# Attention of the second sequence: three of each head's four key blocks transposed by VectorE and a trip through DRAM, in place of two

## The chip, the cores and the metric

The kernel runs on one core of one Trainium2 chip. The time is device microseconds of one execution, the median over runs. Before the change it is 2035.41 us, with three runs from 2034.75 to 2035.72 us.

A core has five engines, each with an instruction stream of its own that runs in order: TensorE (PE, with its weight loads PEld), VectorE (DVE), ScalarE (ACT), GpSimd (POOL) and SyncE (SP). They wait for one another through semaphores. DMAs are issued by an engine (here by SP and POOL) and land later.

## The reference

Two sequences of 512 tokens by 1024 channels go through one encoder layer each, with the same weights: half a step of a SwiGLU network, a token mixer, half a step of a second SwiGLU network, and a final norm. The mixer is the part that matters here:

```
proj = h @ w_in
aq, ak, av, mq, mk, mv, gate_pre, o_pre, g_att, g_mlstm = jnp.split(proj, split_at, axis=-1)
...
att = gqa_block_attention(aq, ak, av)          # 8 heads, 2 key/value heads, head size 64
mem = mlstm_bidirectional(mq, mk, mv, gate_pre, mlstm_gate_bias, o_pre, mlstm_head_norm)   # 4 heads
merged = jax.nn.sigmoid(g_att) * (att @ w_up_att) + jax.nn.sigmoid(g_mlstm) * (mem @ w_up_mlstm)
x = x + merged @ w_out
```

and in the attention, for each block of 128 queries and each head,

```
s = jnp.einsum('bqkgd,bskd->bkgqs', qi, k, preferred_element_type=jnp.float32) * scale
p = jax.nn.softmax(s, axis=-1).astype(v.dtype)
return jnp.einsum('bkgqs,bskd->bqkgd', p, v)
```

The probabilities `p` come out with the query on the partitions. The product with `v` sums over the keys, so it needs them with the key on the partitions: 512 by 512 probabilities of each head have to be transposed. This transposition is what the change touches.

## The kernel before

**Precision.** Every float32 matrix product is done as three matmuls: an operand is split into a high and a low half (`split`, L713: ACT writes the high half, L715, DVE the rest, L716), and high by high, high by low and low by high are summed in PSUM.

**Weights.** A weight unit is loaded and split once, for the first sequence, and both halves are parked in DRAM (`wpark`). The second sequence only reads them back: `load_w` issues two DMAs on SP (L293), of 512 KB each, high and low, into one of four slots `w`. With few exceptions the list of work units (`go`, `fill`) issues a unit's loads some units ahead of its matmuls.

**The mixer of the second sequence**, `mix(1, ...)`. The projections for queries and keys come first. Then the attention runs as a loop over eight heads h and four slots b. In slot b of iteration h the code does, in this order: `score(h + 1, b)`, i.e. two score matmuls for query block b of the *next* head (L1101), a maximum on DVE (L1104), the exponential on ACT (L1106), a reciprocal on DVE (L1107) and the scaling (L1109 on ACT or L1111 on DVE); some filler matmuls (`among`, L825, single matmuls of gate projections that nothing in the attention waits for); the transposition of key block b of head h; more fillers; and `values`, two matmuls (L1148) of the key block that was transposed one slot earlier, with its high half and then its low half. Eight fillers stand in every slot, 7 and 1 in slot 0, 5 and 3 in the others. After the fourth key block of a head, ACT and DVE drain the accumulator `pso` into `f` (L1162, L1163), and every second head splits it into `att`.

A key block is transposed in one of two ways:

- By PE, `turn_keys`: four 128x128 transposes (L1117) write one PSUM bank `pst`, and `parts` splits the bank into `t` tiles (L715, L716). In the first sequence all four key blocks go this way, in the second key blocks 2 and 3, whose values come first (`KBS`).
- By DVE and DRAM, only in the second sequence, key blocks 0 and 1: `turn_early` lets DVE transpose 32x32 squares (L1129, one instruction for each query block of 128 by 256 values) into the tile `box`. `send` writes `box` to DRAM (`abuf`) with four DMAs on SP (L1133) in slot 1. `fetch`, in slots 0 and 1 of the *next* iteration, reads one key block back by a DMA that POOL issues (L1138), in such an order that the whole block comes out transposed, into a tile `f`; `parts` splits that as above.

After the loop stands a tail: key blocks 0 and 1 of head 7 are fetched and multiplied. Around them the program places the value projection of the mLSTM (L804; 96 matmuls for four accumulators, three in the `mm` banks and one in the `pso` bank, evicted to `Vm` by L1009 on ACT and L866 on DVE). Then come the four heads of the mLSTM, each with the same kind of trip by DVE and DRAM: exponentials (L1306) of `box` tiles that are loaded on SP (L1071, `box<-ebuf`) and added to a table (L1074), products with the scores `qk` (L1292, L1308), transposes on DVE (L1330), eight sends on SP (L1334, `tbuf`), and later the closing matmuls (`mem_out`, L1360). Heads 0 and 1 are prepared first, then the closing matmuls of head 0 run, and so on, with work units for PE between them. `proj_w` (L839) does the attention's merge, in units of 24 or 12 matmuls that share a weight load.

**What sets the order.** Most of the attention's matmuls are pinned in the order of the code (`pin`). A scheduler of the framework places all other instructions on each engine by priorities and its own estimates of time. `t` tiles rotate through 11 buffers, `f` tiles through 4; PSUM has three `mm`, one `pso`, two `pss` and two `pst` banks.

## Time and profile before

| | us |
|---|---|
| median of three runs | 2035.41 |
| profiled execution, its own time | 2037.6 |
| span of the profiled execution | 2035.8 |
| PE busy in the span | 2020.2 |
| DVE busy | 1584.0 |
| ACT busy | 921.5 |
| POOL busy | 111.1 |

The granted clock of the profiled execution is 0.999. The span runs from the first to the last recorded instruction; 1.8 us of the execution's own time lie outside it.

How it is read: a row of the timeline begins with the start in us and the length, then the engine, the line, the operation and the tiles as output<-input with buffer numbers left out, `xN` for N instructions shown as one row, and in brackets the idle time of the engine before it with what ended it. Matmuls overlap in the pipeline, so the length of two of them (0.62 us) is longer than the distance at which they follow each other. A row of the table by stretches (windows) gives the stretch, its length and for each engine the busy time with the count of instructions. Rows of grouped instructions give busy time and mean ns of one, then the idle time just before them.

The second sequence's attention takes from about 1075 to 1188 us of the span; iterations h = 0 to 6 begin at 1087.55, 1098.97, 1110.80, 1122.93, 1136.22, 1148.55 and 1160.40 us, and the last two score matmuls at 1168.88 us.

### The profile page before, as it was taken

What the parts mean: (1) busy time and instruction counts of PE and PEld (TensorE: products, weight loads), DVE (VectorE), ACT (ScalarE), POOL (GpSimd) and SP (SyncE); (2) the same over time, 40 slices, a digit from 0 to 9 for tenths busy, and PEclk for the clock granted to TensorE, in tenths of its full rate; (3) what the DMA queues carried; (4) which work ended last, traced back from release to release, by engine and by line L of the source; (5) the groups of instructions that cost most, each with busy time, mean ns of one, the idle gap of its engine ahead of it and who ended that gap; (6) DMA issues with size and microseconds to landing.
All of it is one profiled execution on the core that took longest, in us unless ns stands there. A gap on an engine that the chain in (4) does not pass through costs nothing.

```text
span 2035.8 us, 26777 instructions
## 1 busy us (share of the span) xinstructions
PE 2020.2 (99%) x9185; PEld 1665.7 (82%) x9185; DVE 1584.0 (78%) x2828; ACT 921.5 (45%) x1675; POOL 111.1 (5%) x148
## 2 busy tenths in 40 slices
PE   9999999999999999999999999999999999999998
PEld 7888888888888888888888877888888888888887
DVE  7988888886797798776566867467798988786797
ACT  7644444442234577653325654245444444442224
POOL 0000000001003000100120000011000000000001
PEclk9999999999999999999999999999999999999999
DMA  9656565799766954868656668877565655689753
GB/s 312 197 171 216 177 218 182 237 334 364 271 214 225 294 169 148 259 208 302 211 166 209 214 189 268 274 228 228 173 206 166 217 177 179 205 332 352 269 196 119
DMA packets 334696, 462.17 MB, mean 227 GB/s; under 512 B 21384, under 2 KB 207840, under 8 KB 333280
## 3 DMA queue, kind: packets, MB, share of 16 engines
q1 hardware_dynamic: 329920, 446.08, 65.8%
q0 software_dynamic: 4480, 14.11, 2.0%
q8 instruction: 72, 1.18, 0.2%
q14 instruction: 64, 0.52, 0.1%
q10 hardware_dynamic: 160, 0.27, 0.0%
HBM read 292.44 MB, written 167.94 MB: 226 GB/s over the span
## 4 chain that ended last, share of the span: by engine, by line
PE 91%; DVE 3%; DMA 3%; ACT 2%; issue 1%; SPq 0%; DVEq 0%; ACTq 0%
PE mm L839 13%; PE pso L374 12%; PE pst L374 12%; PE mm L374 10%; PE mm L632 9%; PE pss L374 6%; PE pst L632 4%; PE pss L632 4%; PE mm L825 4%; PE mm L804 3%; PE pso L632 3%; PE pso L1148 1%; PE pss L1101 1%; PE pst L839 1%; PE pss L839 1%; PE pso L1360 1%
## 5 line engine op out<-in xcount | busy, mean ns | idle before, releaser
L374 PE MATMUL pst<-xc,w 128*128 128x512 f32 x1056 | 253.8, 389 | 1.2 <-ACT t L409 1.2
L374 PEld LDWEIGHTS pst<-xc,w 128*128 128x128 f32 x1056 | 198.1, 188 | 42.7 <-ACT t L409 1.6
L374 PE MATMUL mm<-xc,w 128*128 128x512 f32 x972 | 229.6, 390 | 1.6 <-ACT f L382 1.6
L374 PEld LDWEIGHTS mm<-xc,w 128*128 128x128 f32 x972 | 182.0, 188 | 39.6 <-ACT f L382 2.1
L632 PE MATMUL mm<-rt,w 128*128 128x512 f32 x765 | 178.7, 389 | 0.0
L839 PE MATMUL mm<-xh,w 128*128 128x512 f32 x560 | 176.1, 391 | 1.4 <-DMA w<-wpark 1.4
L332 ACT ACTIVATE w<-t 128x512 fp32r<-128x512 f32 x176 | 106.5, 627 | 135.7 <-issue 63.1
L632 PEld LDWEIGHTS mm<-rt,w 128*128 128x128 f32 x765 | 143.5, 188 | 29.8
L333 DVE TENSOR_TENSOR w<-t,w 128x512 fp32r<-128x512 f32 x176 | 117.8, 688 | 40.9 <-ACT w L332 39.1
L374 PE MATMUL pso<-xc,f 128*128 128x512 f32 x528 | 127.0, 389 | 0.0
L374 PE MATMUL pss<-xc,w 128*128 128x512 f32 x528 | 126.8, 389 | 0.0
L374 PE MATMUL pso<-xc,w 128*128 128x512 f32 x528 | 126.8, 389 | 0.0
L839 PEld LDWEIGHTS mm<-xh,w 128*128 128x128 f32 x560 | 104.8, 188 | 23.7 <-DMA w<-wpark 1.8
L374 PEld LDWEIGHTS pso<-xc,f 128*128 128x128 f32 x528 | 99.0, 188 | 21.0 <-DVE t L413 0.4
L374 PEld LDWEIGHTS pso<-xc,w 128*128 128x128 f32 x528 | 99.1, 188 | 20.6
L374 PEld LDWEIGHTS pss<-xc,w 128*128 128x128 f32 x528 | 99.1, 188 | 20.6
L825 PE MATMUL mm<-xh,w 128*128 128x512 f32 x336 | 111.9, 398 | 0.0
L839 PE MATMUL mm<-xl,w 128*128 128x512 f32 x280 | 109.6, 391 | 0.0
L715 ACT ACTIVATE w<-wr 128x512 fp32r<-128x512 f32 x72 | 45.1, 632 | 138.4 <-PE pso L632 64.8
L278 ACT ACTIVATE w<-wr 128x1024 fp32r<-128x1024 f32 (+1 forms) x64 | 65.3, 1030 | 80.4 <-issue 24.5
L279 DVE TENSOR_TENSOR w<-wr,w 128x1024 fp32r<-128x1024 f32 (+1 forms) x64 | 79.8, 1247 | 26.6 <-ACT w L278 15.7
L715 ACT ACTIVATE w<-t 128x512 fp32r<-128x512 f32 x82 | 51.8, 632 | 107.4 <-PE pst L632 62.4
(457 smaller groups left out, 4080.4 us busy)
## 6 DMA issues: line engine op xcount, KB each, us to landing
rt<-rbuf SPq DMA_DIRECT2D x154, 512.0 KB, 5.4
wpark<-w SPq DMA_DIRECT2D x88, 512.0 KB, 3.6
w<-wpark SPq DMA_DIRECT2D x88, 512.0 KB, 5.3
wr<-in_ffn_w_gate_dram SPq DMA_DIRECT2D x62, 512.0 KB, 5.4
rbuf<-tab SPq DMA_DIRECT2D x102, 256.0 KB, 4.0
wr<-in_ffn_w_up_dram SPq DMA_DIRECT2D x44, 512.0 KB, 4.6
rbuf<-f SPq DMA_DIRECT2D x72, 256.0 KB, 4.2
wr<-in_w_in_dram SPq DMA_DIRECT2D x36, 512.0 KB, 5.7
```

The costliest lines, as they stand in the source:

```text
L278: pin(nc.scalar.activation(hi, raw, AF.Copy))
L279: pin(lo_eng.tensor_tensor(lo, raw, f(hi), op=ALU.subtract))
L332: pin(nc.scalar.activation(t[:, 0], src, AF.Copy))
L333: pin(V_.tensor_tensor(t[:, 1], src, f(t[:, 0]), op=ALU.subtract))
L374: nc.tensor.matmul(p, a[:, k, :], xt[:, b, k, :], start=(first and k == 0 and i == 0), stop=(k == HK_ - 1 and i == 2), skip_group_check=True)
L632: nc.tensor.matmul(p, u[:, a, d * P:(d + 1) * P], r[:, b, ts], start=(first and q == 0 and k == 0), stop=(q == len(us) - 1 and k == 2), sk ...
L715: nc.scalar.activation(hi, src, AF.Copy)
L804: mark(nc.tensor.matmul(p[b][:, :N], a[:, k, bs], w_[:, kl, :], start=(k == 0 and i == 0), stop=(k == KD - 1 and i == 2)), (kl, b, i) == ( ...
L825: pin(nc.tensor.matmul(p[0], a[:, k, :], b, start=(k == 0 and i == 0), stop=(k == n - 1 and i == 2)))
L839: mark(nc.tensor.matmul(p, a[:, k, :], b, start=(k == 0 and i == 0), stop=last), last)
L1101: pin(nc.tensor.matmul(p, qT[:, h, b * P:(b + 1) * P], kv[:, hk * 2 + j, :], start=(j == 0), stop=(j == 1)))
L1148: pin(nc.tensor.matmul(pos[h], Vst[:, kb, h // 4, :], w, start=(kb == KBS[0] and i == 0), stop=(kb == KBS[3] and i == 1)))
```

## The change

A constant `NT = 3` says how many key blocks of a head go by DVE and DRAM in the second sequence; it was a literal 2. Key blocks 0, 1 and 2 go that way now, and only key block 3 is transposed by PE. With it:

- a DVE transpose (`turn_early`) works on 128 by 384 values and not 256; there are as many of them as before;
- the four sends of a head carry 192 KB each and not 128 KB, and `abuf` has twelve rows and not eight;
- `fetch` and the split of the fetched block happen in slots 0, 1 and 2 of the next iteration; the tail has three rounds and not two;
- key block 3 comes first in the sum of the values, then 0, 1 and 2.

One line is added, so that each line number behind it is one higher after the change (L1129 is L1130, L1148 is L1149, and so on). The diff:

```diff
+    NT = 3
...
-        turned = boxes["tile"][:, 0:2, :].rearrange("p c (n i m) -> p (c n) i m", i=4, m=32)
+        turned = boxes["tile"][:, 0:NT, :].rearrange("p c (n i m) -> p (c n) i m", i=4, m=32)
 
         def turn_early(t, b):
-            V_.transpose(turned[:, :, b, :], t[:, 0:2 * P].rearrange("p (n m) -> p n m", m=32))
+            V_.transpose(turned[:, :, b, :], t[:, 0:NT * P].rearrange("p (n m) -> p n m", m=32))
 
         def send(h):
             for a in range(4):
-                nc.sync.dma_start(abuf[h % 2][:, :, a, :].rearrange("n r x -> r n x"),
+                nc.sync.dma_start(abuf[h % 2][0:4 * NT, :, a, :].rearrange("n r x -> r n x"),
                                   turned[32 * a:32 * a + 32].rearrange("r n i m -> r n (i m)"))
...
-        KBS = (2, 3, 0, 1) if s else (0, 1, 2, 3)
+        KBS = (*range(NT, 4), *range(NT)) if s else (0, 1, 2, 3)
...
-                if not s or b > 1:
+                if not s or b >= NT:
                     pp = h, b, turn_keys(Ps, b)
                 elif h:
                     pp = h - 1, b, fetch(h - 1, b)
...
-        for b in range(2 * s):
+        for b in range(NT * s):
             pp = HA - 1, b, fetch(HA - 1, b)
             among(sum(FILLER))
             values(*last)
             last = pp
...
-    abuf = [dpool.tile([8, 32, 4, P], F32, name=f"abuf{i}") for i in range(2)]
+    abuf = [dpool.tile([4 * NT, 32, 4, P], F32, name=f"abuf{i}") for i in range(2)]
```

Only instructions of the second sequence's attention and of the stage just behind it change their places. The rows below are what an engine is given, in its order, each with line, operation, output<-input and shape; tile names carry the number of the buffer, so that the same tile can be followed within one program, but not from one program to the other.

**VectorE, iteration 5.** The first row is the maximum of a score block of the next head, `t_12xx` the four probability blocks, `f_12xx` a fetched block (of head 4, in iteration 5). Before, from slot 3 of iteration 4 on:

```order
L1104 TENSOR_REDUCE asm_10058<-pss_10055 128x1
L1129 STREAM_TRANSPOSE box_5278<-t_1224_9955 128x8x32
L1129 STREAM_TRANSPOSE box_5278<-t_1232_9987 128x8x32
L716 TENSOR_TENSOR att_9329<-f_1212_9900,att_9329 128x512
L1107 RECIPROCAL asm_10058<-asm_10058 128x1
L1129 STREAM_TRANSPOSE box_5278<-t_1239_10025 128x8x32
L716 TENSOR_TENSOR t_1252_10082<-pst_10076,t_1251_10081 128x512
L1104 TENSOR_REDUCE asm_10094<-pss_10091 128x1
L1129 STREAM_TRANSPOSE box_5278<-t_1247_10060 128x8x32
L1107 RECIPROCAL asm_10094<-asm_10094 128x1
L1111 TENSOR_SCALAR t_1256_10096<-t_1256_10096,asm_10094 128x512
L716 TENSOR_TENSOR t_1259_10112<-f_1257_10109,t_1258_10111 128x512
```

After, from the maximum of slot 1 of iteration 5 on:

```order
L1105 TENSOR_REDUCE asm_10098<-pss_10095 128x1
L1130 STREAM_TRANSPOSE box_5278<-t_1220_9934 128x12x32
L1130 STREAM_TRANSPOSE box_5278<-t_1229_9967 128x12x32
L1130 STREAM_TRANSPOSE box_5278<-t_1236_10005 128x12x32
L1130 STREAM_TRANSPOSE box_5278<-t_1243_10032 128x12x32
L716 TENSOR_TENSOR t_1255_10088<-f_1253_10085,t_1254_10087 128x512
L1108 RECIPROCAL asm_10098<-asm_10098 128x1
L716 TENSOR_TENSOR t_1262_10116<-f_1260_10113,t_1261_10115 128x512
```

The four transposes of a head, spread over slot 3 and the next iteration's slot 0 before, stand one behind the other in its slot 1 now, between the maximum and the low half of the first fetched block.

**TensorE, the same place after.** `pss_10095` are the scores whose maximum stands first above; `t_1254` and `t_1255` are the high and the low half of that fetched block.

```order
L1102 MATMUL pss_10095<-kv_8555,qT_8558 128x512 x2
L825 MATMUL mm_10046<-xh_8370,w_9838 128x512
L825 MATMUL mm_10046<-xl_8371,w_9838 128x512
L825 MATMUL mm_10046<-xh_8370,w_9838 128x512 x2
L825 MATMUL mm_10046<-xl_8371,w_9838 128x512
L825 MATMUL mm_10046<-xh_8370,w_9838 128x512 x2
L825 MATMUL mm_10046<-xl_8371,w_9838 128x512
L1149 MATMUL pso_10092<-t_1254_10087,kv_8555 128x512
L1149 MATMUL pso_10092<-t_1255_10088,kv_8555 128x512
```

Here PE's order is as it was: two score matmuls, eight fillers, the high half and the low half. What is gone in each head are the four transposes of key block 2 in slot 2.

**VectorE, from head 7's last PE-transposed block to the last accumulator's drain.** Before:

```order
L716 TENSOR_TENSOR t_1317_10367<-pst_10361,t_1316_10366 128x512
L1163 TENSOR_TENSOR f_1318_10372<-pso_10331,f_1319_10373 64x512
L716 TENSOR_TENSOR t_1322_10382<-pst_10376,t_1321_10381 128x512
L716 TENSOR_TENSOR t_1326_10391<-f_1324_10388,t_1325_10390 128x512
L1074 TENSOR_TENSOR box_5278<-box_5278,tab_4218 128x512
L716 TENSOR_TENSOR t_1329_10399<-f_1327_10396,t_1328_10398 128x512
L1308 SCALAR_TENSOR_TENSOR t_1334_10436,dn_10431<-pss_10432,t_1334_10436 128x128
L1163 TENSOR_TENSOR f_1318_10372<-pso_10385,f_1330_10406 64x512
```

After:

```order
L716 TENSOR_TENSOR t_1317_10346<-pst_10340,t_1316_10345 128x512
L1164 TENSOR_TENSOR f_1318_10351<-pso_10317,f_1319_10352 64x512
L867 TENSOR_TENSOR Vm_10610<-mm_10501,Vm_10610 128x512
L867 TENSOR_TENSOR Vm_10610<-mm_10502,Vm_10610 128x512
L867 TENSOR_TENSOR Vm_10610<-mm_10503,Vm_10610 128x512
L1075 TENSOR_TENSOR box_5278<-box_5278,tab_4218 128x512
L716 TENSOR_TENSOR t_1322_10358<-f_1320_10355,t_1321_10357 128x512
L1075 TENSOR_TENSOR box_5278<-box_5278,tab_4218 128x512
L716 TENSOR_TENSOR t_1326_10367<-f_1324_10364,t_1325_10366 128x512
L716 TENSOR_TENSOR t_1329_10375<-f_1327_10372,t_1328_10374 128x512
L1309 SCALAR_TENSOR_TENSOR t_1334_10412,dn_10407<-pss_10408,t_1334_10412 128x128
L1164 TENSOR_TENSOR f_1318_10351<-pso_10361,f_1330_10382 64x512
```

Three evictions of the value projection (`Vm<-mm`) and two additions on `box` stand ahead of the low halves of head 7's fetched blocks now; before, the evictions stood behind the last accumulator's drain. ACT's order has changed alike: three `Vm<-mm` stand ahead of the high halves of head 7.

**TensorE at the same place.** Before, head 7's values are strewn among the L804 matmuls of the `mm` banks:

```order
L1148 MATMUL pso_10385<-t_1325_10390,kv_8555 128x512
L804 MATMUL mm_10526<-w_10519,xh_8370 128x512 x2
L804 MATMUL mm_10526<-w_10519,xl_8371 128x512
L1148 MATMUL pso_10385<-t_1326_10391,kv_8555 128x512
L1148 MATMUL pso_10385<-t_1328_10398,kv_8555 128x512
L804 MATMUL mm_10527<-w_10519,xh_8370 128x512 x2
L804 MATMUL mm_10527<-w_10519,xl_8371 128x512
L1148 MATMUL pso_10385<-t_1329_10399,kv_8555 128x512
L804 MATMUL mm_10525<-w_10522,xh_8370 128x512 x2
```

After:

```order
L804 MATMUL mm_10503<-w_10529,xh_8370 128x512 x2
L804 MATMUL mm_10503<-w_10529,xl_8371 128x512
L1149 MATMUL pso_10361<-t_1321_10357,kv_8555 128x512
L1149 MATMUL pso_10361<-t_1322_10358,kv_8555 128x512
L1149 MATMUL pso_10361<-t_1325_10366,kv_8555 128x512
L1149 MATMUL pso_10361<-t_1326_10367,kv_8555 128x512
L1149 MATMUL pso_10361<-t_1328_10374,kv_8555 128x512
L1149 MATMUL pso_10361<-t_1329_10375,kv_8555 128x512
L804 MATMUL pso_10504<-w_10492,xh_8370 128x512 x2
```

The last six value matmuls stand together, behind all L804 matmuls of the three `mm` banks and ahead of those of the `pso` bank. Ten of the L804 matmuls have moved into the attention, into slot 1 of iteration 6, ahead of the first fetched block of head 5 (eight ahead of its high half, two between the halves).

**SyncE, the mLSTM's first two heads.** `tbuf_259` are sends of head 0's transposes, `tbuf_260` head 1's, `wpark_7582` and `wpark_7617` weight units of the merge. Before:

```order
L1334 DMA tbuf_259<-qt_10499 32x8x128 x4
L293 DMA w_10732<-wpark_7582 128x1024 x2
L1334 DMA tbuf_260<-qt_10714 32x8x128 x4
L1334 DMA tbuf_260<-qt_10715 32x8x128 x4
L293 DMA w_10762<-wpark_7617 128x1024 x2
```

After:

```order
L1335 DMA tbuf_259<-qt_10475 32x8x128 x4
L293 DMA w_10708<-wpark_7582 128x1024
L1335 DMA tbuf_260<-qt_10690 32x8x128 x4
L1335 DMA tbuf_260<-qt_10691 32x8x128 x4
L293 DMA w_10708<-wpark_7582 128x1024
L293 DMA w_10738<-wpark_7617 128x1024 x2
```

The low half of unit `wpark_7582` stands behind the eight sends to `tbuf_260` now, where both halves stood ahead of them.

## The prediction

> **What bounds the kernel now.** I read the page first, for the engines' shares and the chain that ended last, then the windows of the iterations and of the stage behind them.
>
> ```profile
> PE 2020.2 (99%) x9185; PEld 1665.7 (82%) x9185; DVE 1584.0 (78%) x2828; ACT 921.5 (45%) x1675; POOL 111.1 (5%) x148
> PE 91%; DVE 3%; DMA 3%; ACT 2%; issue 1%; SPq 0%; DVEq 0%; ACTq 0%
> ```
>
> PE is busy nearly all the time and carries 91% of the chain. DMA's 3% of the chain already say that there are places where a load ends last. The windows are iterations 1, 3 and 4 of the loop over heads and the last stretch before the mLSTM's first closing matmuls (columns: stretch, length, then PE, PEld, DVE, ACT, POOL busy with counts, clock, DMA share, GB/s).
>
> ```profile
> 1098.97:1110.80 11.83, 11.83 (x58) 9.80 (x57) 8.68 (x21) 8.40 (x19) 1.25 (x2) 1.00 0.67 193
> 1122.93:1136.22 13.29, 12.64 (x60) 10.10 (x59) 11.98 (x32) 9.52 (x21) 1.24 (x3) 1.00 0.60 183
> 1136.22:1148.55 12.33, 12.33 (x62) 10.13 (x61) 11.21 (x29) 8.73 (x20) 1.11 (x2) 1.00 0.65 186
> 1217.68:1231.30 13.62, 12.21 (x52) 9.79 (x53) 3.26 (x5) 1.58 (x3) 1.60 (x3) 1.00 0.98 315
> ```
>
> In an iteration PE has no gap, but for 0.65 us in iteration 3, and DVE is close behind: 8.68 of 11.83 us, 11.21 of 12.33. In the last stretch it is otherwise: DVE and ACT idle, PE stands for 1.41 us, and the DMA engines are full (0.98). So PE's work is time in the attention, if DVE still delivers when PE asks; behind it a late load already stops PE.
>
> **What is removed: 32 PE transposes.** For each of eight heads one set of four goes.
>
> ```profile
> 1105.85 0.60 PE L1117 MATMUL pst<-ident,t 128*128 128x128 f32 x4
> 1106.20 0.71 PE L825 MATMUL mm<-xh,w 128*128 128x512 f32 x2
> 1106.75 0.40 PE L825 MATMUL mm<-xl,w 128*128 128x512 f32 x1
> 1178.95 6.12 PE mm L804 x27
> ```
>
> Matmuls overlap, so I take distances. Twenty-seven full matmuls take 6.12 us in the chain, 0.227 each. From the first transpose to the third filler behind it are 0.90 us, of which two fillers are 0.45; a set costs 0.45. Eight sets: **-3.6 us**, 3.15 of it (seven sets) ahead of the last score pair and 0.45 behind it. The split of a key block is the same for both ways: 686 against 688 ns on DVE, 594 against 625 on ACT.
>
> ```profile
> L1129 DVE STREAM_TRANSPOSE box<-t 128x256 f32<-128x256 f32 x32 | 12.7, 424 | 0.9 <-ACT t L1109 0.8
> L225 DVE STREAM_TRANSPOSE f<-R 128x512 f32<-128x512 f32 x1 | 0.7, 712 | 0.0
> L716 DVE TENSOR_TENSOR t<-pst,t 128x512 fp32r<-128x512 f32 x16 | 11.0, 686 | 1.6 <-ACT t L715 1.5
> L716 DVE TENSOR_TENSOR t<-f,t 128x512 fp32r<-128x512 f32 x16 | 10.9, 688 | 8.1 <-ACT t L715 8.1
> L715 ACT ACTIVATE t<-f 128x512 fp32r<-128x512 f32 x16 | 10.0, 625 | 6.1 <-DMA f<-abuf 6.1
> L715 ACT ACTIVATE t<-pst 128x512 fp32r<-128x512 f32 x16 | 9.5, 594 | 1.5 <-PE pst L1117 1.3
> ```
>
> **What is added on DVE.** No row shows a transpose of 384 values. It lies between the 256 (424 ns) and the 512 (712 ns); halfway is 568, 144 ns more. Thirty-two of them are 4.6 us of DVE work. Bounds are 424 (nothing) and 712 (9.2 us). An iteration of the loop has over 1 us of free DVE time and needs 0.58 more, so the sum alone would be hidden. The place decides.
>
> *In the attention.* The order shows that each head's four transposes now stand in one burst in slot 1, between the maximum of that slot's scores and the low half (L716) of the first fetched block. PE reaches that block's low half eleven matmuls behind the start of the scores (two scores, eight fillers, the high half): 11 x 0.227 = 2.5 us. PE's order is pinned: it waits there if DVE is late, and everything behind it on PE waits too. When is DVE ready?
>
> ```profile
> 1107.44 0.62 PE L1101 MATMUL pss<-kv,qT 128*128 128x512 f32 x2
> 1108.10 0.69 DVE L1104 TENSOR_REDUCE asm<-pss 128x1 f32<-128x512 f32 x1
> 1158.76 0.67 DVE L1104 TENSOR_REDUCE asm<-pss 128x1 f32<-128x512 f32 x1
> 1159.36 1.08 DVE L1129 STREAM_TRANSPOSE box<-t 128x256 f32<-128x256 f32 x3
> 1109.88 1.42 DVE L1129 STREAM_TRANSPOSE box<-t 128x256 f32<-128x256 f32 x4
> 1111.29 0.69 DVE L716 TENSOR_TENSOR t<-pst,t 128x512 fp32r<-128x512 f32 x1
> 1125.60 0.65 DVE L716 TENSOR_TENSOR t<-pst,t 128x512 fp32r<-128x512 f32 x1
> 1126.30 0.50 PE L1148 MATMUL pso<-t,kv 128*128 128x512 f32 x1 [0.65 <-DVE t L716]
> ```
>
> The maximum starts 0.66 us behind the scores (1108.10 - 1107.44), since it reads them. A transpose behind a maximum starts 0.60 later (1159.36 - 1158.76). Four transposes of 256 in a row took 1.41 (1109.88 to 1111.29); with 4 x 0.144 they take 1.98, rounded down to 1.95 for overlap. From the split's start to the matmul that reads it are 0.70 (1125.60 to 1126.30). Sum: 0.66 + 0.60 + 1.95 + 0.70 = 3.9 us. PE asks at 2.5, and so waits 1.4. With transposes of 256 the wait would be 0.85, of 512 2.0. In iterations 1 and 3 the burst stands ahead of the maximum, behind a scaling or an att split; I give them the same 1.4, as I see nothing that makes them much better. Iterations 1 to 5: 5 x 1.4 = 7.0. In iteration 6 the block is covered by the ten L804 matmuls that were moved in front of it, and iteration 7 belongs to the tail. Of the wait before, 0.65 in the row above (all of iteration 3's 13.29 - 12.64 us) is part of that, and 7.0 - 0.65 = **+6.35 us** is what I take, with 3.6 (256) and 9.4 (512) as ends.
>
> *Behind the waiting instructions.* Behind the burst on DVE stand the reciprocal and the scaling of the same slot's scores; they have three slots until a PE transpose reads them. SP's four sends of a head carry half as much again, and POOL issues three fetches a head, not two. Do these reach PE? The fetch chain of head 7 gives the distance:
>
> ```profile
> 1172.80 0.44 DVE L1129 STREAM_TRANSPOSE box<-t 128x256 f32<-128x256 f32 x1
> 1173.27 1.84 SPq L1133 DMA_DIRECT2D abuf<-box  x4
> 1177.73 1.06 POOL L1138 DMA_DIRECT2D f<-abuf  x2 [9.59 <-DVE f L1163]
> 1183.70 1.26 ACT L715 ACTIVATE t<-f 128x512 fp32r<-128x512 f32 x2 [6.09 <-DMA f<-abuf]
> ```
>
> From the last transpose's end (1173.24) to ACT's first split are 10.5 us, to its end (half of 1.26) 11.1. A burst ends about 3.2 us behind slot 1's scores, so the block is there at 14.3, or at some 15.2 if each of the sends, issue and landing, takes half a microsecond more. The next iteration's PE asks one iteration (11.83 - 0.45 + 1.4 = 12.8) and 2.3 later, at 15.1. It is close, but the low half waits for the next burst until 12.8 + 3.9 = 16.7 anyway. I charge nothing; without that cover it is up to 1.5 us a head.
>
> ```profile
> f<-abuf POOLq DMA_DIRECT2D x16, 256.0 KB, 4.1
> ```
>
> A fetch lands 4.1 us after its issue in the median. [...]
>
> [...]
>
> **The tail** (time from the last score pair, 1168.88; the row with 6.76 is from the chain, the others from the timeline).
>
> ```profile
> 1168.88 0.63 PE L1101 MATMUL pss<-kv,qT 128*128 128x512 f32 x2
> 1186.95 0.39 PE L1148 MATMUL pso<-t,kv 128*128 128x512 f32 x1
> 1188.06 0.70 DVE L1163 TENSOR_TENSOR f<-pso,f 64x512 f32<-64x512 f32 x1 [1.59 <-ACT f L1162]
> 1202.83 1.31 DVE L866 TENSOR_TENSOR Vm<-mm,Vm 128x512 fp32r<-128x512 f32 x2
> 1202.83 0.59 ACT L1009 ACTIVATE Vm<-mm 128x512 fp32r<-128x512 f32 x1
> 1214.77 4.05 SPq L1334 DMA_DIRECT2D tbuf<-qt  x8
> 1219.38 6.76 DMA w<-wpark
> 1226.18 0.73 PE L839 MATMUL mm<-xh,w 128*128 128x512 f32 x2 [1.41 <-DMA w<-wpark]
> 1231.30 2.88 PE L1360 MATMUL pso<-t,Vm 128*128 128x512 f32 x12
> ```
>
> 1. PE's order now has 95 matmuls and two transpose sets from here to the end of the `mm` banks' L804: 95 x 0.227 + 0.9 + 0.3 for a short wait at head 6's first block = 22.7. Then PE meets head 7's last six value matmuls in one group.
> 2. DVE may do their low halves only behind three evictions, which need those banks. ACT goes first (0.59), so DVE's last one starts at about 23.5 and takes 0.65 (1.31 for two). Then two additions on `box` and three low halves stand before the last value matmul, at the distance of 0.60 that DVE showed above: 23.5 + 0.65 + 5 x 0.60 = 27.2. Six matmuls after 22.7 would have been done at 24.1; they are done at 27.4.
> 3. The next L804 use the `pso` bank, which ACT (0.59) and DVE (0.70) drain first: PE goes on at 28.9, another 1.5 us behind.
> 4. The drain L1163 starts at 28.2 and not at 19.2 (1188.06). From it to head 1's `tbuf` sends were 26.7 us (1214.77 - 1188.06), of which 1.5 are the three evictions done earlier now: 28.2 + 26.7 - 1.5 = 53.4.
> 5. The low half of unit `wpark_7582` is issued behind these eight sends (4.05): 57.5. Its landing I take as 5.5, between the median of the 25 such loads around here, 4.7, and the 6.76 of the chain's row, so it is there at 63.
>
> ```profile
> w<-wpark SPq DMA_DIRECT2D x25, 512.0 KB, 4.7
> ```
>
> 6. PE needs it 98 matmuls behind step 3, at 28.9 + 22.2 = 51.1 if nothing else were late: waits of 11.9 us in all, some of them earlier, at score banks and mLSTM values that are late for the same reason.
> 7. Then 46 matmuls (10.4) up to L1360: 73.4. Before it was 1231.30 - 1168.88 = 62.4, so +11.0. The ten L804 in iteration 6 are not in the 95 and cost their 2.3 there: **+13.3 us**, the eighth set included.
>
> Step 5 carries it. If the load were not behind the sends, or if head 1's chain did not hang on L1163, steps 2 and 3 would stay: 3.3 + 1.5 of waits, less the 1.41 that the last stretch has before, less a set: +2.9. At the other end, a landing of 6.76 and 2 us more in the chain, since both `box<-ebuf` loads of head 0 now follow the last send, give +17.
>
> **Sum.** -3.15 + 6.35 + 13.3 = **+16.5 us**. The profiled execution took 2037.6 for a span of 2035.8; it would be 2054.1, span 2052.3. It stands 2.2 above the median of 2035.41; added to that median: 2051.9, given as **2052.0 us**.
>
> **The rivals.**
> - *Transposes off PE are a plain gain (faster).* DVE catches up, no wait is added: -3.6, 2031.8. It decides if the burst behind the maximum is under 0.5 us, where the rows say 1.4 at least for 256. For it: DVE has free time in each iteration. Chance 0.05.
> - *Only the attention waits.* The tail is hidden by the mLSTM's L1292 and merge matmuls: -3.6 + 6.35 = +2.75, 2038.2. Against it: the load's place behind the sends. Chance 0.07.
> - *Only the tail waits.* The scheduled burst turns out early enough, since its inputs are ready before slot 1 and DVE may run ahead of PE: -3.15 + 13.3 = +10.2, 2045.6. Against it: DVE runs in order, and the maximum ahead of the burst needs the scores. Chance 0.18, which also takes in a tail of half its size.
> - *The fetch chain too.* The cover is gone and seven heads pay 1.5 more: +27, 2062. For it: 15.2 against 15.1. Chance 0.07.
> - *The forecast* has the remaining 0.63; with the attention from 3.6 to 9.4 and the tail from +10 to +17, it spans 2035.41 - 3.15 + 13.6 = 2045.9 at the low end and 2058 where not all of both goes wrong at once.
>
> About 0.2%, 4 us, is what a measurement of this kernel can tell from no change. Faster by more needs more than the first rival gives (3.6): 0.02. Within it lie the rest of that rival, 0.03, and the second: 0.10. Slower: 0.88. The range 2043 to 2058 leaves out the first two rivals and the fetch chain, about 2 in 10.
>
> **What would show it.** Right: PE waits of 1 to 2 us at L1149 in slot 1 of iterations 1 to 5, ended by DVE L716; DVE transposes near 570 ns; a wait of 3 to 4 us at head 7's last values and of over 5 at an L840 ended by `w<-wpark`; the first L1361 at about 73 us behind the last scores. Wrong: iterations shorter than before; the load of `wpark_7582` not the last to release PE; transposes near 710 ns; or `f<-abuf` as the releaser of ACT's splits in most iterations.

## The result, and the profile after

The change makes the kernel slower. The median is 2056.52 us (four runs, 2055.36 to 2058.43) against 2035.39 of the kernel before in the same sitting, a ratio of 1.0105 with a 95% interval of 1.0088 to 1.0123: +21.1 us, where +16.5 were forecast. The profiled execution took 2055.36 us for a span of 2053.6, at a granted clock of 0.995.

Three points in the second sequence's mixer cut the two traces alike: the first score matmuls of the attention, its last score pair (1168.88 us before, 1172.66 after), and the first closing matmul of mLSTM head 0 (L1360, after the change L1361).

| stretch, us | before | after | difference | forecast |
|---|---|---|---|---|
| span's start to first scores | 1077.41 | 1075.36 | -2.05 | 0 |
| A: first scores to last pair | 91.47 | 97.30 | +5.83 | +5.47 |
| B: last pair to first closing of head 0 | 62.42 | 78.17 | +15.75 | +11.0 |
| first closing of head 0 to that of head 3 | 69.97 | 69.75 | -0.22 | 0 |
| from there to the last matmul | 727.49 | 725.97 | -1.52 | 0 |

The forecast for A is -3.15 + 6.35 + 2.27 (the ten L804 that moved there), for B the 11.0 of its step 7. The first and the last row are not the change's: the 2.05 us lie ahead of all that it touches, 1.64 of them in the first 69 us of the span, and the 1.52 in what follows the mixer. The mixer alone is 21.4 us longer, which fits the medians. What follows is about A and B.

The page of the kernel after, the lines of engines and of the chain:

```profile
PE 2024.1 (99%) x9153; PEld 1666.5 (81%) x9153; DVE 1586.0 (77%) x2828; ACT 921.8 (45%) x1675; POOL 115.2 (6%) x156
PE 92%; DVE 4%; DMA 1%; ACT 1%; issue 1%; SPq 0%; DVEq 0%; POOLq 0%; ACTq 0%
```

PE has 32 instructions fewer and is *longer* busy, by 3.9 us. Busy time is no measure of work here, as will be seen: 26 matmuls follow each other at 0.427 us in place of 0.227. The stretches of iterations 1, 3 and 4, and of the last stretch from PE's stop to the first closing matmul:

```profile
1095.83:1108.21 12.38, 11.68 (x53) 9.33 (x52) 8.45 (x18) 7.40 (x18) 1.06 (x2) 1.00 0.72 216
1121.52:1135.51 13.99, 12.52 (x56) 9.48 (x55) 11.45 (x31) 9.33 (x21) 1.69 (x3) 1.00 0.71 218
1135.51:1148.82 13.31, 12.13 (x57) 9.74 (x56) 11.00 (x25) 8.65 (x19) 1.60 (x3) 1.00 0.68 203
1231.76:1250.83 19.07, 12.29 (x47) 10.03 (x47) 2.67 (x5) 0.60 (x1) 1.60 (x3) 0.82 0.97 317
```

Each iteration is longer though PE has less to do in it: the difference of the first two numbers of a row is PE's idle time, 0.70, 1.47 and 1.18 us, where before iterations 1 and 4 had none. The timeline shows where PE stands in the attention, and the burst that it stands for:

```profile
1101.93 0.50 PE L1149 MATMUL pso<-t,kv 128*128 128x512 f32 x1 [0.70 <-DVE t L716]
1114.78 0.51 PE L1149 MATMUL pso<-t,kv 128*128 128x512 f32 x1 [1.18 <-DVE t L716]
...
1128.98 0.50 PE L1149 MATMUL pso<-t,kv 128*128 128x512 f32 x1 [0.77 <-DVE t L716]
1142.08 0.51 PE L1149 MATMUL pso<-t,kv 128*128 128x512 f32 x1 [1.18 <-DVE t L716]
1155.94 0.50 PE L1149 MATMUL pso<-t,kv 128*128 128x512 f32 x1 [1.30 <-DVE t L716]
```

```profile
L1130 DVE STREAM_TRANSPOSE box<-t 128x384 f32<-128x384 f32 x32 | 15.9, 547 | 0.8 <-ACT t L1110 0.8
1111.60 0.69 DVE L1105 TENSOR_REDUCE asm<-pss 128x1 f32<-128x512 f32 x1 [0.42 <-PE pss L1102]
1112.20 1.95 DVE L1130 STREAM_TRANSPOSE box<-t 128x384 f32<-128x384 f32 x4
1114.08 0.65 DVE L716 TENSOR_TENSOR t<-f,t 128x512 fp32r<-128x512 f32 x1
```

Five iterations, five waits at L1149 in slot 1, each ended by DVE's L716: the maximum, the burst of 1.95 us, the low half, then PE. By distances the five slots have grown by 7.09 us in all (0.97 in iteration 1, 1.45 to 1.61 in the others). The idle times in the rows sum to 5.13 only. A sixth wait, 0.29 us for ACT at 1127.71 in iteration 3, is not among them, and the overlap of matmuls is lost at each pause: the one ahead is 0.39 us long and the one behind is followed after 0.33 or 0.34, where matmuls follow at 0.227 otherwise, so that a pause costs some 0.28 us beside its idle time. Behind the last pair PE stands at six places:

```profile
1196.49 0.50 PE L1149 MATMUL pso<-t,kv 128*128 128x512 f32 x1 [1.20 <-ACT t L715]
1197.90 2.85 PE L1149 MATMUL pso<-t,kv 128*128 128x512 f32 x5 [0.91 <-DVE t L716]
1202.16 1.22 PE L804 MATMUL pso<-w,xh 128*128 128x512 f32 x2 [1.41 <-DVE f L1164]
1227.35 0.73 PE L1293 MATMUL pss<-mem 128*128 128x512 f32 x2 [1.18 <-ACT mem L715]
1230.10 1.19 PE L1293 MATMUL pss<-mem 128*128 128x512 f32 x4 [2.01 <-DVE mem L716]
1238.54 1.22 PE L839 MATMUL mm<-xh,w 128*128 128x512 f32 x2 [6.78 <-DMA w<-wpark]
```

The first three are head 7's late values and the drain, the next two head 2's operands, and the last is a weight load, which SP issued only behind head 1's eight sends:

```profile
1229.17 3.90 SPq L1335 DMA_DIRECT2D tbuf<-qt  x8
1233.41 2.93 SPq L293 DMA_DIRECT2D w<-wpark  x5
```

One thing in B was not forecast at all. Windows of 3 us (behind the counts: clock, DMA share, GB/s):

```profile
1195.00:1198.00 3.00, 0.89 (x4) 0.29 (x2) 3.00 (x6) 2.92 (x8) 0.00 (x0) 0.98 0.00 0
1198.00:1201.00 3.00, 2.75 (x5) 1.23 (x5) 1.86 (x5) 0.85 (x4) 0.00 (x0) 0.50 0.00 0
...
1237.00:1240.00 3.00, 1.46 (x4) 1.18 (x5) 0.00 (x0) 0.00 (x0) 0.00 (x0) 0.50 1.00 337
...
1243.00:1246.00 3.00, 3.00 (x15) 2.47 (x14) 0.00 (x0) 0.41 (x1) 0.00 (x0) 1.00 0.94 341
```

In the second and the third window the granted clock is 0.50. The trace's clock events give two such stretches, 10.24 us from 1197.85, right behind two of PE's pauses, and 6.83 us from 1235.40, in its longest. Matmuls follow each other there at 0.427 us and not 0.227; 18 and 8 of them are so slowed, 26 x 0.2 = 5.2 us of PE time, an estimate from these distances. The kernel before has none in its mixer.

One name in the text above the prediction was wrong: `wpark_7582` and `wpark_7617` are the query and key projections of mLSTM head 3 (they meet `xh`, not `att`), not units of the merge. The merge's first unit is the next one, `wpark_7154`. The expectation of e2 has the same slip. The line to look for was L839 and not L840, since it stands ahead of the added line. No number hung on either.

### The profile page after: what moved, and what is told of

Its sections match the earlier page's. It is cut to its first block, busy times and chain, and to the rows that moved or that the text cites. A ratio compares the mean times of both kernels' runs of the same rounds, so it can differ in the third digit from the quotient of the medians.

```text
span 2053.6 us, 26734 instructions
## 1 busy us (share of the span) xinstructions
PE 2024.1 (99%) x9153; PEld 1666.5 (81%) x9153; DVE 1586.0 (77%) x2828; ACT 921.8 (45%) x1675; POOL 115.2 (6%) x156
## 3 DMA queue, kind: packets, MB, share of 16 engines
q8 instruction: 72, 1.18, 0.2%
## 4 chain that ended last, share of the span: by engine, by line
PE 92%; DVE 4%; DMA 1%; ACT 1%; issue 1%; SPq 0%; DVEq 0%; POOLq 0%; ACTq 0%
PE mm L839 14%; PE pso L374 12%; PE pst L374 12%; PE mm L374 11%; PE mm L632 8%; PE pss L374 6%; PE pst L632 4%; PE pss L632 4%; PE mm L804 4%; PE mm L825 3%; PE pso L632 3%; PE pso L1149 1%; PE pst L839 1%; PE pss L839 1%; PE pso L1361 1%; PE pss L1102 1%
## 5 line engine op out<-in xcount | busy, mean ns | idle before, releaser
L839 PE MATMUL mm<-xh,w 128*128 128x512 f32 x560 | 177.7, 394 | 6.8 <-DMA w<-wpark 6.8
L332 ACT ACTIVATE w<-t 128x512 fp32r<-128x512 f32 x176 | 106.5, 627 | 135.7 <-issue 63.1
L839 PEld LDWEIGHTS mm<-xh,w 128*128 128x128 f32 x560 | 105.6, 189 | 29.4 <-DMA w<-wpark 7.2
L839 PE MATMUL mm<-xl,w 128*128 128x512 f32 x280 | 110.1, 393 | 0.0
```

The lines of the kernel that those rows point to most:

```text
L332: pin(nc.scalar.activation(t[:, 0], src, AF.Copy))
L839: mark(nc.tensor.matmul(p, a[:, k, :], b, start=(k == 0 and i == 0), stop=last), last)
```

## The experiments

In all of them "behind" means the order of issue on one engine: a helper adds an edge without a wait between two instructions, and the framework's scheduler places the rest around it. What stands behind a # in the cuts of code is a note for the reader, and a cut shows the part of an edit that matters.

```diff
+    def behind(i, *first):
+        for j in first:
+            tc.add_manual_dep(i.ins, j.ins.name, mybir.DependencyInfo(mybir.DependencyClass.NoSync,
+                              mybir.DependencyReason.DATA), reason="order")
+        return i
```

The kernel before, run beside each, had medians from 2034.6 to 2036.3, so ratios compare best. C is the stretch from the first closing matmul of head 0 to that of head 1, 20.92 us before and 20.93 after.

| run | median | ratio, 95% interval | A | B | C |
|---|---|---|---|---|---|
| before | 2035.39 | 1 | 91.47 | 62.42 | 20.92 |
| after | 2056.52 | 1.0105 (1.0088 to 1.0123) | 97.30 | 78.17 | 20.93 |
| e1_burst_slot0 | 2053.49 | 1.0087 (1.0070 to 1.0104) | 94.44 | 76.80 | 20.92 |
| e2_load_first | 2055.59 | 1.0095 (1.0079 to 1.0110) | 97.39 | 71.69 | 27.72 |
| e3_drain_first | 2048.75 | 1.0063 (1.0048 to 1.0078) | 97.36 | 70.23 | 20.92 |
| e4_pe_kept_busy | 2055.29 | 1.0094 (1.0079 to 1.0109) | 97.33 | 77.44 | 20.95 |
| e5_before_burst_slot1 | 2044.23, one run | | 96.70 | 65.73 | 20.93 |
| e6_burst_and_drain | 2045.21 | 1.0046 (1.0030 to 1.0063) | 93.22 | 69.91 | 20.94 |
| e7_head7_two | 2058.12 | 1.0107 (1.0092 to 1.0122) | 97.31 | 78.92 | 20.90 |
| e8_burst_drain_load | 2036.74 | 1.0003 (0.9994 to 1.0012) | 93.26 | 59.42 | 23.47 |
| e9_burst_early | 2045.05 | 1.0048 (1.0035 to 1.0061) | 101.78 | 59.72 | 25.03 |
| e10_before_load_first | 2038.80 | 1.0016 (1.0007 to 1.0025) | 91.45 | 59.52 | 27.29 |
| e11_sends_by_gpsimd | 2049.26 | 1.0063 (1.0050 to 1.0075) | 97.30 | 69.28 | 20.90 |
| e12_burst_drain_gpsimd | 2033.96 | 0.9989 (0.9980 to 0.9998) | 93.15 | 59.50 | 20.93 |

**e1: the burst one slot earlier.** The four transposes stand in slot 0 ahead of that slot's reciprocal, and slot 1's maximum behind the low half of the first fetched block.

```diff
-                if s and (h, b) != (HA - 1, 3) and b in (3, 0):
...
+                if s and b == 0:
+                    for i in range(2 if h == 0 else 0, 4):
+                        turn_early(Ps[i], i)
...
+            if s and h > 1 and b == 0:
+                behind(i_, *early_[-4:])          # i_: the reciprocal
...
+            if s and h > 1 and b == 1:
+                behind(i_, low[-1])               # i_: the maximum
```

> The changed kernel (three key blocks by VectorE), with VectorE's order alone altered in iterations 1 to 6: the burst of four transposes stands in slot 0, ahead of the reciprocal of that slot's scores, and the low half of the first fetched block stands ahead of slot 1's maximum. PE's order in the attention is the same. Theory (the place of the burst makes the waits): the five waits at L1149 in slot 1 go or fall under 0.3 us each, the last score pair comes 5 to 6.5 us earlier behind the start of the attention, the tail is as it was; 2056.5 becomes about 2050.5. Rival (the trip through DRAM is late by itself, the burst only hides it): the waits stay at 1 us or more, now ended by ACT's split or the DMA f<-abuf, and the time stays within 1.5 us of 2056.5.

A fell by 2.86 us, about half of what was expected. The waits of iterations 1 and 2 are gone; from iteration 3 on the timeline has

```profile
1125.42 0.50 PE L1161 MATMUL pso<-t,kv 128*128 128x512 f32 x1 [0.29 <-ACT t L721]
1126.43 0.50 PE L1161 MATMUL pso<-t,kv 128*128 128x512 f32 x1 [0.52 <-DVE t L722]
...
1153.35 0.50 PE L1161 MATMUL pso<-t,kv 128*128 128x512 f32 x1 [1.18 <-DVE t L722]
```

In iterations 3 and 5 the split of `att` waits 0.70 us for ACT ahead of the burst, so the burst is late again. The same transposes with the same cost, in another place, make PE wait less: the place is a cause. e6 puts that split behind the burst, and the last of these waits is 0.49 and not 1.18. A wait of 0.73 in iteration 5, for the drain of an accumulator (DVE's L1176), stays as it was in e6.

**e5: the burst without the width.** The kernel before, two blocks by DRAM, with its four transposes of 256 in slot 1 behind the maximum.

```diff
+                if s and b == 1 and 0 < h < HA - 1:
+                    for i in range(4):
+                        turn_early(Ps[i], i)
+                    for i in early_[-4:]:
+                        behind(i, tops_[0])
+                    behind(low[-1], early_[-1])
```

> The kernel before (two key blocks by VectorE, transposes of 256 values), with the four transposes of a head put in one burst in slot 1 of iterations 1 to 6, behind that slot's maximum and ahead of the low half of the first fetched block, which is where they stand in the changed kernel. The tail's order moves too, so only the stretch from the attention's first scores to its last is read (91.5 us in the kernel before). Theory (the place makes the waits, at any width): PE waits 0.6 to 1.0 us at the low half in each of iterations 1 to 5, the stretch grows by 3 to 4 us to about 95. Rival (the greater width of 384, or the larger DMAs, make the waits): the stretch stays at 91.5 within 0.5 us.

```profile
1104.00 0.50 PE L1156 MATMUL pso<-t,kv 128*128 128x512 f32 x1 [0.65 <-DVE t L722]
1116.80 0.51 PE L1156 MATMUL pso<-t,kv 128*128 128x512 f32 x1 [0.65 <-DVE t L722]
```

The waits come up at the same matmul with the old width, and shorter (0.63 to 0.77, and one of 0.23 more). A grew by 5.23, where 3 to 4 were expected: by distances 4.67 in slot 1 of iterations 1 to 5, 0.9 us each, and 0.92 in iteration 6, where the scheduler moved four L804 matmuls, with 0.36 less in the other slots. So by this one run the place alone makes 4.67 us of the 7.09, and the greater width with what hangs on it the rest. B grew too, so that the 8 us of this one run can't be put down to the waits of A.

**e3: the drain first.** The evictions of the value projection stand behind head 7's drain, on ACT and on DVE.

```diff
+                    if s:
+                        behind(i_, drain[0])
+                        behind(j_, drain[1])
```

> The changed kernel, with the four evictions of the value projection behind the drain of head 7 on ACT and on VectorE; as a side effect the low half of the merge's first unit now stands ahead of the sends, as in the run above, so this run is to be read against that one. Theory (head 7's last values wait for splits that stand behind evictions): the waits of 1.2 and 0.9 us there go, PE's clock stays at full speed in that place, and the time is 3 to 5 us below the run with only the load moved, about 2044. Rival (those splits are late because of their data, the third fetch of head 7): the waits stay and the time is that of the run with only the load moved, within 1 us.

B fell by 7.94 us. The drain is at 24.6 us behind the last pair and not at 28.75, the pauses at head 7's values and the first half-clock stretch are gone. The load wait is still there in full:

```profile
1233.51 0.80 PE L845 MATMUL mm<-xh,w 128*128 128x512 f32 x1 [6.85 <-DMA w<-wpark]
```

The scheduler set both halves of `wpark_7582` ahead of head 1's sends here, but the next unit, `wpark_7617`, stands behind them still, and PE waits for that one instead. So the run tells what the drain costs, with a load wait as long as before. It is 6.8 us under e2, where 3 to 5 were expected.

**e2: the load first.** Head 1's sends stand behind the loads of the next three units on SP.

```diff
+            for i in sent[1]:
+                behind(i, loads["up", 0, 0])
```

> The changed kernel, with the eight sends of mLSTM head 1 put behind both halves of the merge's first weight unit on SP (the two units behind it come ahead of the sends too). Theory (the low half is late only because it stands behind the sends): the wait of 6.8 us at that unit goes, and with it the second stretch at half clock; 2056.5 falls by 7 to 9 us to about 2048.5. Rival (the DMA engines are full there, or the next load or head 1's own chain is late anyway, so that another wait takes its place): it falls by less than 3 us.

The load wait is gone and B is 6.5 shorter, but C is 6.8 longer, and the time fell by 0.9 us only. PE stands at head 2's scores instead:

```profile
1258.93 2.93 PE L1299 MATMUL pss<-mem 128*128 128x512 f32 x6 [4.15 <-DVE t L1315]
```

I read this as the rival at first: the load wait covers a chain that is late anyway. The order on DVE says otherwise. After the change, the first product of head 2's scores (on `pss_10896`) stands ahead of head 0's normalisation (`row`):

```
L225 STREAM_TRANSPOSE f_1397_10869<-t_1395_10864 128x512
L1309 SCALAR_TENSOR_TENSOR t_1402_10900,dn_10895<-pss_10896,t_1402_10900 128x128
L226 TENSOR_REDUCE row_10870<-f_1397_10869 128x16
```

In e2 it stands behind the whole normalisation and its transpose back:

```
L264 STREAM_TRANSPOSE f_1397_10869<-row_10870 128x512
L1081 TENSOR_TENSOR box_5278<-box_5278,tab_4218 128x512
L1384 SCALAR_TENSOR_TENSOR box_5278<-box_5278,hn,f_1397_10869 128x512
L1081 TENSOR_TENSOR box_5278<-box_5278,tab_4218 128x512
L1315 SCALAR_TENSOR_TENSOR t_1402_10900,dn_10895<-pss_10896,t_1402_10900 128x128
```

The scheduler, told that the sends come later, took head 2's inputs for later too. TensorE has a part of head 2's score matmuls behind matmuls of the merge then, too. So e2 changed more than the load's place, and so did e8, e9 and e10, which have the same edit. e11 is the clean form of it.

**e10: the same edit on the kernel before.**

> The kernel before (two blocks through DRAM) with nothing changed but SyncE's order: the sends of mLSTM head 1 stand behind the next three weight units. If the wait for weights in the mixer's last part (1.41 us in before) is a cost of its own, it goes and the kernel gives 2034.7 plus or minus 0.6 us. Rival: the wait covers the lateness of mLSTM head 2's scores as it did in e2_load_first; TensorE then waits there as long and the kernel stays at 2036 plus or minus 0.5 us.

Neither: B is 2.9 shorter, without the 1.41 wait, but C is 6.4 longer and the kernel 0.16% slower. DVE's order has changed as in e2.

**e4: PE kept busy.** Fifteen matmuls into a bank that nobody reads stand ahead of head 7's last six value matmuls, where PE would pause.

```diff
+            if b == 1:
+                extra_work.extend(idle_work(15))
...
+            behind(extra_work[0], ended[2])
```

> The changed kernel with 15 matmuls more, whose result nobody reads, ahead of head 7's last six value matmuls, where PE waited: 3.4 us of work in a place where 2.1 us of idle time and five matmuls at half clock lay. Theory (the granted clock fell because PE stood still, and the matmuls at half clock lengthen the tail): the clock stays at 1.0 there, the 14 matmuls behind run at 0.227 us again, and the time falls by 1 to 4 us, to about 2054. Rival (the drop has another cause, or the matmuls at half clock lie beside the mLSTM's chain and cost nothing): the time stays at 2056.5 or grows by up to 3.4 us.

The first half-clock stretch is gone (first row; the same place read 0.50 above), and yet B is 0.73 shorter only:

```profile
1198.00:1201.00 3.00, 3.00 (x14) 2.05 (x12) 2.80 (x7) 1.59 (x5) 0.00 (x0) 1.00 0.00 0
1237.00:1240.00 3.00, 3.00 (x8) 2.32 (x9) 0.00 (x0) 0.00 (x0) 0.00 (x0) 0.50 1.01 367
```

So PE's standing still causes the drop in this place. PE resumes behind the load 64.0 us behind the last pair, not 65.9. The drain is no earlier (29.0, not 28.75), but from it to head 1's sends it takes 25.8 us and not 27.8, while the orders of ACT and DVE are the same: so 1.9 us is what the first drop costs the load, through the mLSTM chain. The second drop, 13.65 us long now, takes 1.1 of it back.

**e7: head 7 with two blocks.** Its key block 2 is turned by PE, so that the tail has two rounds again.

```diff
+            KBS = (3, 2, 0, 1) if s and h == HA - 1 else KBS_
...
+            pp = HA - 1, b, turn_keys(old, 2) if b == 2 else fetch(HA - 1, b)
```

> The changed kernel, with head 7 alone as before: its key block 2 is turned by PE again, and two blocks are fetched in the tail, not three. The orders on VectorE and ACT still have the three evictions ahead of the low halves. Theory (the place of the evictions makes head 7 late, not the third fetch): the tail to the first closing matmuls keeps its 78 us within 1.5, and the time stays within 1.5 us of 2056.5. Rival (the third trip of head 7 through DRAM makes the tail late): the tail shortens by 5 us or more, and the time falls below 2052.

No better, as expected: 1.6 us more by the medians, with intervals that overlap, and B at 78.92. The third round is not what makes the tail late.

**e6, e8: one after the other.** e6 is e1 with the `att` split behind the burst, and e3; e8 is e6 and e2.

```diff
+                    while halves:
+                        behind(halves.pop(), early_[-1])
```

> The changed kernel with the order of the first run (burst in slot 0), every second head's att split put behind the burst as well, in iteration 7 too, and with the evictions behind head 7's drain as in the third run. Theory (what is left of the waits in the first run comes from the att split and its wait for ACT ahead of the burst; head 7's burst comes 1.4 us earlier, and the mLSTM's chain with it): the stretch to the last scores is 92 to 93.5 us, where the first run had 94.4, and the time is the third run's 2048.8 less 4 to 5 in the attention and 1 in the tail, about 2043. Rival (VectorE has too much to do in these iterations, so the waits only wander): the stretch is 94.4 or more and the time 2046 or more.

> The kernel of the run with burst and drain, and in addition the load order of the second run (the sends of mLSTM head 1 behind the next three weight units). Theory as it stands after the second run (the chain of the mLSTM heads, which starts with head 7's drain, ends the tail, and a load that comes earlier only lets PE wait at head 2's scores): the time is that of the run with burst and drain within 1.5 us, and idle time moves from the load to the scores of head 2. Rival (the load was what ended the wait once the drain is earlier): 4 to 7 us less.

e6 gains 11.3 us, within the scatter what e1 (3.0) and e3 (7.8) gain apart; it stays 2 us above the 2043 expected, with A where it was expected. e8 is level with the kernel before, so the expectation that it would stay with e6 failed: with the drain early, moving the load is worth 8.5 us, more than its rival's 4 to 7, where it was worth 0.9 in e2, though C is still 2.5 too long.

**e9: the burst earlier still.** e8 with two transposes in slot 3, and all four ahead of slot 0's maximum.

```diff
-                    for i in range(2 if h == 0 else 0, 4):
+                    for i in range(2, 4):
...
+                    if s and b == 3:
+                        for i in range(2):
+                            turn_early(nxt[i], i)
```

> The kernel of e8_burst_drain_load with the burst of four transposes moved further forward: two of the copies into bfloat16 are made in slot 3 of the iteration before and the four transposes stand ahead of slot 0's maximum on VectorE. Place theory: the waits left in iterations 1 to 5 of the attention (0.2 to 0.75 us each in e8) shrink, the stretch from the attention's start to the last score matmuls falls from 93.3 by 1.5 to 2 us, and the kernel gives 2035 plus or minus 1.5 us. Rival: the same 1.95 us of VectorE time then holds up slot 0's reciprocal and the drain of slot 3 instead, the waits wander and the kernel stays at 2036.7 plus or minus 1.

A is 8.5 us longer than in e8. The waits are back and longer, up to 1.58 us, most of them ended by ACT's high halves now. Three half-clock stretches of 3.41 us come up, two behind these waits and one in C. The rival was right that the waits would wander, but neither side expected 2045; why ACT is late there was not followed further. (The expectation speaks of copies into bfloat16; what moves is the float32 transposes.)

**e11: head 1's sends by GpSimd.** The same aim as e2, but SP's order needs no edge.

```diff
+                    i = (nc.gpsimd if h == 1 else nc.sync).dma_start(
...
+            for i in sent[1]:
+                behind(i, *fetched)               # GpSimd's own four fetches of head 0
```

> The changed kernel with the eight sends of mLSTM head 1 issued by GpSimd, behind its four fetches of head 0, and not by SyncE; so the weight loads stand behind nothing on SyncE, and, other than in e2_load_first, the order on TensorE, ScalarE and VectorE stays as it was (there the planner had also put the evictions of head 2's scores behind head 0's normalisation on VectorE). Theory as written in step 5 of the prediction: the load wait is a cost of its own; TensorE's wait of 6.78 us and part of the second stretch at half clock go, head 2's scores follow without a new wait, and the kernel falls from 2056 by 6 to 9 us, to 2048 plus or minus 1.5. Rival, as read from e2: the load wait only covers the lateness of the mLSTM chain; a wait of 3 to 5 us comes up at head 2's scores, and the kernel stays at 2055.5 plus or minus 1.

PE's order and ACT's are those of the changed kernel to the last instruction, DVE's but for one place of a `box` addition. The median falls by 7.3 us, B by 8.89, and C stays. PE's last waits ahead of the first closing matmul are now

```profile
1229.92 0.73 PE L1299 MATMUL pss<-mem 128*128 128x512 f32 x2 [1.22 <-ACT mem L721]
1232.66 1.20 PE L1299 MATMUL pss<-mem 128*128 128x512 f32 x4 [2.01 <-DVE mem L722]
```

with no load and no half clock behind them. So the load behind the sends is a cost of its own, 6.78 us of wait and some 1.6 at half clock (8 x 0.2); the other 0.5 of the 8.89 is open. No other wait came up in its place.

**e12: all three places put right.** e6 with head 1's sends by GpSimd.

> The kernel of e6_burst_and_drain with the sends of mLSTM head 1 by GpSimd as in e11_sends_by_gpsimd, and nothing else moved. If the load wait is a cost of its own, TensorE's waits of 6.84 and 0.81 us go and its last half-clock stretch with them, and the 2.10 us wait that e8_burst_drain_load kept at head 2's scores does not come up: 2034.5 plus or minus 1.5 us, level with the kernel before or a little under it. Rival: the wait at head 2's scores comes up again with 2 us or more: 2036.7 us or slower.

This is as expected, and the lowest of all: 0.9989 of the time before, 22.6 us under the changed kernel. One at a time e1, e3 and e11 gain 3.0, 7.8 and 7.3, which is 4.5 less; together, and with the `att` split moved, they leave no half clock in A, B or C. All waits of PE over 0.2 us in A and B:

```profile
1126.06 0.49 PE L1164 MATMUL pso<-t,kv 128*128 128x512 f32 x1 [0.30 <-ACT t L721]
1126.79 0.50 PE L1164 MATMUL pso<-t,kv 128*128 128x512 f32 x1 [0.23 <-DVE t L722]
1139.38 0.51 PE L1164 MATMUL pso<-t,kv 128*128 128x512 f32 x1 [0.39 <-DVE t L722]
1149.27 0.73 PE L1164 MATMUL pso<-t,kv 128*128 128x512 f32 x2 [0.70 <-DVE f L1179]
1153.03 0.50 PE L1164 MATMUL pso<-t,kv 128*128 128x512 f32 x1 [0.51 <-DVE t L722]
1195.27 0.73 PE L810 MATMUL pso<-w,xh 128*128 128x512 f32 x2 [1.41 <-DVE f L1179]
1216.88 1.92 PE L1306 MATMUL pss<-mem 128*128 128x512 f32 x6 [0.23 <-ACT mem L721]
```

They sum to 3.8 us, where those of the kernel before sum to 2.3 (0.65 and 0.23, and the 1.41 for a load); so they take back 1.5 of the 3.6 that the 32 transposes saved. A and B together are 1.24 us shorter than before. With the interval from 0.4 to 4.1 us the gain over the kernel before is small but there. That it comes of the transposes is not shown: e12 has also lost that kernel's own wait of 1.41 for a load, and the kernel before with its sends by GpSimd was not run.

## Why the prediction was right, and where it was off

Sign, range and mechanism held; the size was 4.6 us short, nearly all of it in B.

- **Removed transposes.** Confirmed: each set was worth 0.45 us, and seven of them shorten A.
- **The burst in the attention.** Confirmed: five waits at L1149 in slot 1, 7.09 us by distances where 5 x 1.4 = 7.0 stood, at 547 ns a transpose (568) and 1.95 us a burst. e1 and e5 show that the place makes most of them. That iteration 1 would wait as long as the others was coarse: 0.97 against 1.45 to 1.61. The 0.65 us taken off was a misreading: the wait at 1126.30 is in slot 0 of iteration 3, at a block that PE transposed, and slot 0 as a whole is 0.1 us longer after the change. And two value matmuls that moved behind the last pair, 0.49 us by distance, were left out of A. So A is -3.15 - 0.49 + 7.09 + 2.27 + 0.1 = 5.82, against 5.83 measured; that 5.47 came so close is luck in part, as these two errors nearly cancel.
- **The fetch chain** as a rival: ACT waits three times for `f<-abuf` in A, 2.9 us together, but none of PE's waits there follows from it. It stayed covered or cost nothing that shows.
- **Steps 1 to 4.** The drain came at 28.75 us behind the last pair (28.2). From it to head 1's sends it took 27.8 and not 25.2: 2.6 too little. By e4, where it takes 25.8, 1.9 of this is the first half-clock stretch, in which the scores of the mLSTM heads run that the sends wait for; the rest is open.
- **Step 5,** "Step 5 carries it": right. The load was issued behind the sends and ended PE's longest wait, its landing at 65.9 us (63). e11 takes it away and nothing else, and B loses 8.89 us. That a step 2 and 3 without it would leave only +2.9 was too low, though: e11 still has B at 69.28, where 62.42 + 2.9 - 2.27 = 63.1 would follow. The 3.2 us of waits for head 2's operands, which step 6 counted with the load, and 3.6 (18 x 0.2) of the first half-clock stretch remain, against 1.3 less in steps 2 and 3 (3.5 us of waits, not 4.8): 68.6. The last 0.7 is open.
- **Step 7,** "46 matmuls (10.4)": they took 12.3, since eight of them ran at half clock.

So the term that failed is +11.0 for B. Its errors add up to what was measured: 73.4 + 0.55 (drain) + 2.6 (chain) - 0.4 (landing) + 1.9 (half clock) = 78.05, against 78.17. The cause common to most of it is a price per matmul, 0.227, that I took for constant: where PE was busy for 0.89 of 3.00 us, and behind the wait of 6.78, the clock fell to 0.50, and the matmuls behind took 0.427.

The rivals "a plain gain" and "only the attention waits" and "only the tail waits" are out by A and B. With the three places in order, e12 is 2.3 us faster than the kernel before, of which it stays open how much is the transposes'.

## What to carry to other kernels

PE is the bound here, and the work that was moved off it cost by its place in the other engines' queues, not by its amount: the added DVE work, 32 x 123 ns = 3.9 us, costs nothing that shows in e12, and one burst ahead of a due split, one drain behind three evictions and one load behind eight sends cost the 22.6 us by which e12 is faster. Read the in-order queues around the moved work first, and mend the order before judging the idea. And when an experiment shifts an order by an edge, compare every engine's order, not only the one that the edge names: e2 seemed to refute a step that was right.

## What the hardware showed that was not expected

The clock that was granted to PE fell to 0.50 behind short pauses. The stretches at half clock are 3.41 (e9), 6.83 and 10.24 (the changed kernel) and 13.65 us long (e4) in the mixers of these runs, and a 128x512 matmul follows the last at 0.427 us there instead of 0.227. A wait of 6.78 us led to one, as might be thought, but so did 1.20 and 0.91 us with one matmul between (PE busy 0.89 of 3.00 us in the window above), and in e9 waits of 1.58 and 0.30; single waits of 1.18 to 1.41 didn't. The pauses of about 1.2 and of 2.01 us for head 2's operands come in six traces: half clock follows them within a step of 3.41 us in e1, e2, e4 and e7, in the changed kernel only behind the longer wait for the load, and in e11 not at all.

In these traces, what tells them apart is where the pauses fall on a raster of time. In each of the 14 traces all half-clock stretches, that at the kernel's end included, begin whole multiples of 3.413 us apart, as if on a raster of that step: in the changed kernel 1197.85 and 1235.40 are 37.55 us apart, eleven steps. In the step ahead of the first (1194.44 to 1197.85) PE is busy for 1.35 us, a share of 0.40. The pause of 2.01 us there falls on two steps, and PE is busy for 1.75 us (0.51) of the one and 1.66 (0.49) of the other; in e1 one step holds all of it, with a share of 0.41. Over the 14 traces, from 1075 to 1310 us, all 13 steps at full clock with PE busy for less than 0.46 were followed by half clock, 5 of the 9 between 0.46 and 0.54, and none above. What decides between 0.46 and 0.54 is open; the ends of matmuls in a trace are modelled, so the shares are not exact. The raster lies at another place of the kernel in each trace: carried there from the half-clock stretches, its first point behind the attention's first scores comes some 0.3 us behind them before the change and 3.0 after it. So the same pauses may cost more in one execution than in another.
